# A delta-rule stage in which matmuls of constants are placed by another count

## The chip, the cores and the metric

The kernel runs on one core of a Trainium2 chip. The metric is the time of one launch on the device, in microseconds (us). PE is TensorE's matmul unit and PEld its loading of weights, DVE is VectorE, ACT ScalarE, POOL GpSimd, and SP the engine whose queue issues the DMAs. The clock granted to PE has two levels, 1.2 and 2.4 GHz; the profile gives it as a share of the higher one.

## The reference

Two blocks stand behind each other. The first has two layers on 256 context and 256 latent tokens of width 1024: each is a half FFN, a mixer and a second half FFN, with modulated norms. Layer 0's mixer is the gated delta rule, layer 1's a windowed attention. The second block has a mixer of three branches, a cross-attention to a memory of 256 tokens and an MLP. The change lies in the delta rule:

```python
def _gated_delta_chunked(q, k, v, g, beta):
    ...
    gc = jnp.cumsum(_to_chunks(g, DN_CHUNK), axis=-1)
    decay = jnp.exp(jnp.where(causal, gc[..., :, None] - gc[..., None, :], -jnp.inf))
    kb = k * beta[..., None]
    lower = jnp.where(strict, jnp.einsum('nhcid,nhcjd->nhcij', kb, k) * decay, 0.0)
    rhs = jnp.concatenate([v * beta[..., None], kb * jnp.exp(gc)[..., None]], axis=-1)
    uw = lax.linalg.triangular_solve(lower, rhs, left_side=True, lower=True, unit_diagonal=True)
    ...
    def step(state, inp):
        u_c, w_c, qk_c, qg_c, kd_c, a_c = inp
        v_new = u_c - jnp.einsum('nhik,nhkv->nhiv', w_c, state)
        o = jnp.einsum('nhik,nhkv->nhiv', qg_c, state) + jnp.einsum('nhij,nhjv->nhiv', qk_c, v_new)
        state = state * a_c[..., None, None] + jnp.einsum('nhjk,nhjv->nhkv', kd_c, v_new)
        return state, o
```

There are 8 heads of 128, each run forwards and backwards over 512 tokens.

## The kernel before

All instructions are issued by a planner that runs when the program is built (`Driver`, line 191 is the call through which every operation is recorded). Pieces of work are Python generators: streams with a priority, and jobs, which are taken one after the other and carry the large weight matmuls. The planner keeps a clock of its own for each engine (`Clocks.t`), adds a cost of its own for each operation, and lets the first stream go on whose inputs are ready by these clocks; where none can, the job goes on, and where the job can't either, PE's clock is moved to the next time at which something can (`Driver.run`). So the costs and the constants of the planner set the order of the instructions on each engine; on the chip the engines run these orders and wait for each other by semaphores. Weights in float32 are split into a high and a low part (ACT casts, DVE subtracts, `split_w`, line 433), and products of them are three matmuls each.

The delta-rule stage, as far as it matters here: `dn_subst` loads the diagonal 32x32 blocks of four heads' lower triangles (bx<-ld) and an identity (bx<-in_eye), and `dn_steps` inverts them on DVE in 31 steps of two operations. `dn_head` then loads these inverses (t<-xd) and the triangles (t<-ld), and widens the inverse to 64 and to 128 rows by small matmuls on PE: products of 32x32, a "solve" of many 32x32 matmuls, and two sets of 64x64; it then loads keys, queries and values (t<-s, t<-q). `dn_chain` runs the state through four chunks of 128 tokens, for two directions of a head, with up to four heads under way: matmuls with a state tile s, 128x128, whose results DVE and ACT take up before the next can start. Heads 0 to 3 go first, heads 4 to 7 behind. `dn_norm` and `dn_finish` norm and gate the result, and the output projection (128x512) follows. Beside this, jobs fill PE: the projections of z and six of the eight products of the memory's keys (`mem_k`, 128x256).

From the end of the projections to the last output projection `drv.hot` holds two constants, a tile of ones and the identity (lines 1635 and 1662). While it does, `keep_busy` may issue a float32 matmul of them, 128x128, whose result nobody reads, into a free PSUM tile:

```python
if self.hot is None or until - now < HOT_GAP or self.clk.cols.get(int(now / TICK), 0) >= HOT_COLS or not self.q["ps"]:
    return False
```

It is called at one place, where no stream and no job can go on.

## Time and profile before

| | |
|---|---|
| median of three runs | 2732.3 us (2727.0 to 2738.47) |
| the profiled execution | 2734.16 us |
| its span | 2732.4 us |
| PE, DVE, ACT, POOL busy | 2654.7, 1929.0, 1258.0, 102.2 us |
| the delta-rule stage's part spoken of here | 640.0 to 833.6 us |

The profile is that of one execution. Times in its rows are us from the start of the span unless marked ns; a row of a timeline merges instructions of one kind that follow each other, and the brackets at its end give the idle time before it and what ended it. A float32 matmul leaves two records on PE and two on PEld. In rows of groups "x" is the number of records.

### The profile page before, as it was taken

What the parts mean: (1) busy time and instruction counts of PE and PEld (TensorE: products, weight loads), DVE (VectorE), ACT (ScalarE), POOL (GpSimd) and SP (SyncE); (2) the same over time, 40 slices, a digit from 0 to 9 for tenths busy, and PEclk for the clock granted to TensorE, in tenths of its full rate; (3) what the DMA queues carried; (4) which work ended last, traced back from release to release, by engine and by line L of the source; (5) the groups of instructions that cost most, each with busy time, mean ns of one, the idle gap of its engine ahead of it and who ended that gap; (6) DMA issues with size and microseconds to landing.
All of it is one profiled execution on the core that took longest, in us unless ns stands there. A gap on an engine that the chain in (4) does not pass through costs nothing.

```text
span 2732.4 us, 45388 instructions
## 1 busy us (share of the span) xinstructions
PE 2654.7 (97%) x17414; PEld 2327.2 (85%) x17414; DVE 1929.0 (71%) x3897; ACT 1258.0 (46%) x2799; POOL 102.2 (4%) x114
## 2 busy tenths in 40 slices
PE   6999999999889999999999998999999899999999
PEld 4888888888788888889888886799978899999999
DVE  4778767887868488876433357775588998986763
ACT  3322236764345322224423245564476667555662
POOL 0000000200010000000000002000010211000000
PEclk8999999999879999999999999999999999999999
DMA  6657732668442455673322222165555444554554
GB/s 247 231 194 254 261 123 97 225 200 226 152 151 89 135 206 210 225 257 104 108 93 95 94 90 85 47 214 184 172 167 165 156 153 172 181 188 160 178 193 139
DMA packets 194058, 452.57 MB, mean 166 GB/s; under 512 B 33472, under 2 KB 78624, under 8 KB 193840
## 3 DMA queue, kind: packets, MB, share of 16 engines
q1 hardware_dynamic: 193840, 449.66, 49.2%
q8 instruction: 137, 2.24, 0.3%
q14 instruction: 81, 0.66, 0.1%
HBM read 418.65 MB, written 30.94 MB: 165 GB/s over the span
## 4 chain that ended last, share of the span: by engine, by line
PE 89%; DVE 5%; ACT 2%; DMA 2%; issue 1%; SPq 1%; POOL 0%; DVEq 0%; ACTq 0%; POOLq 0%
PE ps L191 89%; DVE t L191 2%; ACT t L191 1%; DVE rs L191 1%; DVE n L191 1%; SPq L236 1%; ACT s L191 1%; DMA xres<-in_xT 0%; DVE s L191 0%; DMA bx<-ld 0%; DVE xres L191 0%; DMA t<-in_memT 0%; DVE bx L191 0%; ACT L191 0%; DVE acc L191 0%
## 5 line engine op out<-in xcount | busy, mean ns | idle before, releaser
L191 PE MATMUL ps<-t,t 128*128 128x256 f32 (+4 forms) x14610 | 2386.7, 326 | 34.0 <-DVE t L191 19.6
L191 PEld LDWEIGHTS ps<-t,t 128*128 128x128 f32 (+2 forms) x14610 | 2068.6, 186 | 308.3 <-issue 28.7
L191 DVE TENSOR_TENSOR t<-raw,t 128x512 fp32r<-128x512 f32 x1124 | 736.8, 685 | 76.5 <-ACT t L191 69.9
L191 ACT CAST t<-raw 128x512 fp32r<-128x512 f32 x1124 | 630.4, 610 | 261.9 <-DMA raw<-in_ffn_w 177.9
L191 ACT CAST t<-t 128x512 fp32r<-128x512 f32 (+2 forms) x144 | 68.3, 493 | 438.5 <-DVE t L191 438.3
L191 DVE TENSOR_TENSOR t<-t,ps 128x512 f32<-128x512 f32 (+1 forms) x104 | 64.7, 628 | 240.0 <-PE ps L191 239.9
L191 DVE CUSTOM_DVE_ANT_0 t<-row,bx,c_early 128x1024 bf16<-128x1024 f32 x128 | 163.9, 1281 | 54.2 <-DMA row<-in_ada_r 53.7
L191 DVE SCALAR_TENSOR_TENSOR xres<-ps,modG,xres 128x256 f32<-128x256 f32 x216 | 97.2, 479 | 119.1 <-PE ps L191 118.0
L191 ACT ACTIVATE t<-ps 128x512 f32<-128x512 f32 (+3 forms) x161 | 74.9, 466 | 205.3 <-PE ps L191 195.9
L191 POOL TENSOR_TENSOR t<-t,c_late 128x512 f32<-128x512 f32 (+2 forms) x58 | 68.2, 1194 | 1742.4 <-ACT t L191 1106.9
L191 DVE CUSTOM_DVE_ANT_0 row<-row,bx,c_early 128x1024 f32<-128x1024 f32 x96 | 122.9, 1280 | 1.4
L191 DVE TENSOR_TENSOR t<-t,t 128x512 fp32r<-128x512 f32 (+4 forms) x174 | 95.2, 561 | 39.4 <-ACT t L191 39.0
L191 DVE SCALAR_TENSOR_TENSOR t<-ps,c_late,t 128x254 f32<-128x254 f32 (+3 forms) x176 | 112.0, 637 | 12.1 <-ACT t L191 7.0
L191 PE MATMUL ps<-s,t 128*128 128x128 f32 x512 | 88.3, 323 | 12.7 <-ACT s L191 4.5
L191 ACT COPY t<-ps 128x512 f32<-128x512 f32 (+4 forms) x141 | 57.9, 435 | 83.4 <-PE ps L191 77.5
L191 PEld LDWEIGHTS ps<-s,t 128*128 128x128 f32 x512 | 76.5, 224 | 20.5 <-ACT s L191 7.2
L191 DVE SCALAR_TENSOR_TENSOR xres<-t,c_late,xres 128x256 f32<-128x256 f32 x150 | 87.5, 583 | 3.1
L191 ACT ACT_TABLE_LOAD x58 | 74.4, 1283 | 2.7 <-PE ps L191 1.7
L191 PE MATMUL ps<-c_early,t 128*128 128x128 f32 (+1 forms) x374 | 57.9, 280 | 6.3 <-ACT t L191 3.4
L191 ACT ACTIVATE n<-xres 128x256 f32<-128x256 f32 x90 | 35.9, 414 | 59.9 <-DVE xres L191 58.0
L191 ACT ACTIVATE t<-ps,c_late 128x256 f32<-128x256 f32 (+1 forms) x64 | 37.7, 589 | 54.2 <-PE ps L191 53.9
L191 DVE TENSOR_TENSOR acc<-acc,n 128x256 f32<-128x256 f32 x102 | 42.7, 422 | 27.1 <-ACT n L191 23.9
(181 smaller groups left out, 1378.0 us busy)
## 6 DMA issues: line engine op xcount, KB each, us to landing
raw<-in_ffn_w SPq DMA_DIRECT2D x240, 512.0 KB, 4.3
row<-in_ada_r SPq DMA_DIRECT2D x128, 512.0 KB, 4.4
raw<-in_w_in SPq DMA_DIRECT2D x81, 512.0 KB, 3.5
raw<-in_dn_w SPq DMA_DIRECT2D x33, 512.0 KB, 4.0
raw<-in_w_up SPq DMA_DIRECT2D x32, 512.0 KB, 4.0
raw<-in_w_down SPq DMA_DIRECT2D x32, 512.0 KB, 5.6
raw<-in_ffn_w SPq DMA_DIRECT2D x32, 384.0 KB, 3.6
raw<-in_ada_w SPq DMA_DIRECT2D x16, 512.0 KB, 5.6
```

Of the source, the lines that this page charges most:

```text
L191: r = f(*a, **k)
L236: self.nc.sync.dma_start(out=out, in_=in_)
```

## The change

Where before asks how many columns PE was given in the current one of fixed pieces of the planner's time, the changed planner keeps a list of PE's operations with their columns and sums those that began within the last TICK (a constant of the code). It asks at two places: ahead of every choice of work, where it adds a matmul of the constants if the sum is under HOT_WORK, and in waits of at least HOT_GAP, if it is under HOT_WAIT. In waits the limit was 3600 and the least wait 0.3.

```diff
--- before.py
+++ after.py
@@ -44,8 +44,8 @@
 FG = 1
 NWY = 14
 SPLP = 6
-HOT_COLS = 3600
-HOT_GAP = 0.3
+HOT_WORK, HOT_WAIT = 4000, 5500
+HOT_GAP = 0.25
 HOT_LAG = 1.0
 TICK = 3.4133
 DMA_LAT = 0.75
@@ -110,6 +110,7 @@
     def __init__(self):
         self.t = {"PE": 0.0, "ACT": 0.0, "DVE": 0.0, "POOL": 0.0, "DMA": 0.0}
         self.log = {}
+        self.recent = deque()
         self.cols = {}
 
     @staticmethod
@@ -135,6 +136,7 @@
         if e == "PE":
 
             tick = int(start / TICK)
+            self.recent.append((start, cost * 2400 * rows))
             self.cols[tick] = self.cols.get(tick, 0) + cost * 2400 * rows
             if self.cols.get(tick - 1, 0) < 3060:
                 cost *= 2
@@ -337,6 +339,8 @@
     def run(self):
         while True:
             now = self.t["PE"]
+            if self.keep_busy(now, HOT_WORK):
+                continue
             first = [s for s in self.streams if s.split] if self.ahead < AHEAD else []
             for s in first + self.streams:
                 if self.ok(s, now, s in first):
@@ -372,24 +376,26 @@
                 cand = [c for c in cand if c > now]
                 if not cand:
                     raise RuntimeError("no stream can go on: " + self.state())
-                if not self.keep_busy(now, min(cand)):
+                if min(cand) - now < HOT_GAP or not self.keep_busy(now, HOT_WAIT):
                     self.t["PE"] = min(cand)
 
-    def keep_busy(self, now, until):
-
-        if self.hot is None or until - now < HOT_GAP or self.clk.cols.get(int(now / TICK), 0) >= HOT_COLS or not self.q["ps"]:
+    def keep_busy(self, now, least):
+
+        r = self.clk.recent
+        while r and r[0][0] < now - TICK:
+            r.popleft()
+        if self.hot is None or sum(c for _, c in r) >= least:
             return False
         i = next((i for i in self.q["ps"] if all(o[4] <= now - HOT_LAG for o in self.clk.log.get(f"ps{i}", ()))), None)
         if i is None:
             return False
-        self.q["ps"].remove(i)
-        self.q["ps"].appendleft(i)
-        t = self.take("hot")
-        a, b = self.hot
-        self.pe.matmul(t[:, 0:P], a, b, start=True, stop=True)
-        self.free(t)
-        self.q["ps"].remove(i)
-        self.q["ps"].appendleft(i)
+        for _ in range(2):
+            self.q["ps"].remove(i)
+            self.q["ps"].appendleft(i)
+            if _ == 0:
+                t = self.take("hot")
+                self.pe.matmul(t[:, 0:P], *self.hot, start=True, stop=True)
+                self.free(t)
         return True
 
     def state(self):
```

By the order of the instructions, PE has 77 matmuls of the constants in place of 32 (in the rows `c_early` holds the identity). Since they move the planner's clock, other work changes places too. Lines below the diff's first part stand two further down in the changed kernel (L193 for L191, L238 for L236). Three places are shown.

PE, the memory's key products at the start of the stage. Before (ps is a PSUM tile, t a tile of weights or of the normed memory, three matmuls to a group):

```order
L191 MATMUL ps_5785<-t_5928,t_5656 128x256 x2
L191 MATMUL ps_5785<-t_5928,t_5657 128x256
L191 MATMUL ps_5973<-c_early,ones 128x128
L191 MATMUL ps_5785<-t_5933,t_5656 128x256 x2
L191 MATMUL ps_5785<-t_5933,t_5657 128x256
L191 MATMUL ps_5785<-t_5952,t_5682 128x256 x2
L191 MATMUL ps_5785<-t_5952,t_5683 128x256
L191 MATMUL ps_5995<-c_early,ones 128x128
L191 MATMUL ps_5785<-t_5957,t_5682 128x256 x2
L191 MATMUL ps_5785<-t_5957,t_5683 128x256
```

Of the change, the same work, up to the first 32x32 products of head 0:

```order
L193 MATMUL ps_5785<-t_5936,t_5656 128x256 x2
L193 MATMUL ps_5785<-t_5936,t_5657 128x256
L193 MATMUL ps_5989<-c_early,ones 128x128
L193 MATMUL ps_5785<-t_5941,t_5656 128x256 x2
L193 MATMUL ps_5785<-t_5941,t_5657 128x256
L193 MATMUL ps_5997<-c_early,ones 128x128
L193 MATMUL ps_5785<-t_5966,t_5682 128x256 x2
L193 MATMUL ps_5785<-t_5966,t_5683 128x256
L193 MATMUL ps_6010<-c_early,ones 128x128
L193 MATMUL ps_6013<-t_5825,t_5829 32x32 x8
L193 MATMUL ps_6014<-t_5826,t_5830 32x32 x8
L193 MATMUL ps_6031<-c_early,ones 128x128
```

Before, 11 groups of key products stand ahead of head 0's 32x32 products, with two matmuls of the constants among them; now five groups, with four.

PE, the last 64x64 set of one head and the first 32x32 products of the next, among the heads 4 to 7 (n holds a product that is passed on, s a state tile). Before:

```order
L191 MATMUL ps_6961<-t_6848,n_6960 64x64 x4
L191 MATMUL ps_6962<-t_6849,n_6960 64x64 x4
L191 MATMUL ps_7099<-s_7103,t_5846 128x128
L191 MATMUL ps_7118<-t_6947,t_6951 32x32 x8
L191 MATMUL ps_7119<-t_6948,t_6952 32x32 x8
L191 MATMUL ps_7099<-s_7136,t_5850 128x128
L191 MATMUL ps_7150<-s_7105,t_5857 128x128
L191 MATMUL ps_7150<-s_7105,t_5856 128x128
L191 MATMUL ps_7118<-t_6949,n_7070 32x32
```

Of the change:

```order
L193 MATMUL ps_7165<-t_7067,n_7122 64x64 x4
L193 MATMUL ps_7166<-t_7068,n_7122 64x64 x4
L193 MATMUL ps_7335<-s_7311,t_5865 128x128
L193 MATMUL ps_7335<-s_7311,t_5864 128x128
L193 MATMUL ps_7341<-t_7262,t_7266 32x32 x8
L193 MATMUL ps_7342<-t_7263,t_7267 32x32 x8
L193 MATMUL ps_7359<-c_early,ones 128x128
L193 MATMUL ps_7361<-c_early,ones 128x128
L193 MATMUL ps_7363<-c_early,ones 128x128
L193 MATMUL ps_7365<-c_early,ones 128x128
L193 MATMUL ps_7367<-c_early,ones 128x128
L193 MATMUL ps_7335<-s_7369,t_5866 128x128
```

Five matmuls of the constants, into one PSUM tile, stand behind the 32x32 products, ahead of the state matmuls that followed them. Strings of eight stand at four more places: two around the first column sums of the keys' norms, one some 20 rows ahead of head 4's first 32x32 products, and one behind those of head 7.

SP's queue, where the load of the identity for heads 4 to 7 stands (raw is a buffer for weights as they come, bx the tiles of the substitution, s and q scratch in DRAM). Before:

```order
L236 DMA bx_5949<-ld_119 128x32x32
L236 DMA raw_6006<-in_dn_w_out 128x512
L236 DMA raw_6094<-in_dn_w_out 128x512
L236 DMA raw_6192<-in_dn_w_out 128x512
L236 DMA bx_5950<-in_eye 128x1024
L236 DMA t_5817<-s_146 128x512
L236 DMA t_5818<-s_147 128x512
L236 DMA t_5821<-s_148 128x512
L236 DMA t_5822<-s_149 128x512
L236 DMA t_5823<-q_122 128x512
L236 DMA t_5824<-q_123 128x512
```

Of the change:

```order
L238 DMA bx_5948<-ld_119 128x32x32
L238 DMA raw_6089<-in_dn_w_out 128x512
L238 DMA t_5825<-s_146 128x512
L238 DMA t_5826<-s_147 128x512
L238 DMA t_5829<-s_148 128x512
L238 DMA t_5830<-s_149 128x512
L238 DMA t_5831<-q_122 128x512
L238 DMA t_5832<-q_123 128x512
L238 DMA raw_6175<-in_dn_w_out 128x512
L238 DMA bx_5949<-in_eye 128x1024
L238 DMA raw_6257<-in_dn_w_out 128x512
```

The load bx<-in_eye stood behind three loads of weights; now it stands behind one, six loads of head 0 and another of weights.

## Rows read from the trace of the kernel before

**Rows 1.** The page, part 2: PE busy and granted clock in 40 slices, in tenths.

```profile
PE   6999999999889999999999998999999899999999
...
PEclk8999999999879999999999999999999999999999
```

**Rows 2.** Stretches of the stage: length, busy by engine (instructions), granted clock, DMA share, GB/s.

```profile
640.00:654.00 14.00, 12.80 (x68) 9.19 (x66) 6.56 (x18) 5.16 (x12) 0.00 (x0) 1.00 1.07 276
654.00:661.10 7.10, 6.76 (x27) 5.88 (x28) 5.78 (x16) 3.31 (x9) 0.00 (x0) 0.52 1.08 280
...
691.00:705.00 14.00, 10.12 (x152) 8.50 (x152) 12.43 (x33) 6.25 (x20) 1.04 (x1) 1.00 0.79 280
705.00:729.10 24.10, 22.70 (x164) 21.12 (x165) 17.00 (x58) 6.00 (x21) 2.11 (x2) 0.58 0.33 87
729.10:749.60 20.50, 17.80 (x174) 16.11 (x175) 18.16 (x60) 6.58 (x22) 0.00 (x0) 1.00 0.49 145
749.60:777.00 27.40, 27.35 (x267) 24.75 (x262) 12.89 (x42) 8.35 (x28) 2.08 (x2) 0.50 0.50 155
777.00:796.90 19.90, 16.34 (x212) 14.14 (x210) 13.55 (x44) 10.81 (x44) 1.04 (x1) 1.00 0.53 159
796.90:804.30 7.40, 5.13 (x76) 4.85 (x78) 1.81 (x9) 3.83 (x18) 0.00 (x0) 0.54 0.25 73
804.30:833.60 29.30, 26.11 (x227) 23.59 (x220) 25.68 (x84) 16.36 (x58) 7.12 (x7) 1.00 0.26 83
833.60:860.00 26.40, 26.40 (x135) 22.07 (x136) 21.76 (x54) 12.51 (x37) 2.91 (x2) 1.00 0.32 110
640.00:833.60 193.60, 171.83 (x1725) 152.54 (x1723) 136.99 (x412) 79.25 (x261) 14.55 (x14) 0.84 0.55 160
```

**Rows 3.** Chain of waits in the stage: start, length, what.

```profile
664.68 8.59 DMA bx<-ld
...
747.89 20.36 PE ps L191 x223
```

**Rows 4.** Timeline of weight loads, 643 to 658 us: start, length, instruction, idle before it.

```profile
644.18 0.30 PEld L191 LDWEIGHTS ps<-c_early,ones 128*128 128x128 f32 x2 [0.25 <-PE ps L191]
...
651.82 0.30 PEld L191 LDWEIGHTS ps<-c_early,ones 128*128 128x128 f32 x2 [0.25 <-PE ps L191]
...
655.87 0.50 PEld L191 LDWEIGHTS ps<-c_early,ones 128*128 128x128 f32 x2 [0.35 <-PE ps L191]
...
657.58 0.50 PEld L191 LDWEIGHTS ps<-c_early,ones 128*128 128x128 f32 x2 [0.35 <-PE ps L191]
```

**Rows 5.** Timeline of PE: the string of 16, two at half clock, one wait.

```profile
643.74 8.57 PE L191 MATMUL ps<-c_early,ones 128*128 128x128 f32 x32
...
723.74 1.49 PE L191 MATMUL ps<-c_early,ones 128*128 128x128 f32 x4
...
799.17 0.87 PE L191 MATMUL ps<-t,t 32*32 32x32 f32 x16 [3.84 <-ACT t L191]
```

**Rows 6.** Groups of PE from 729.1 and from 749.6 us: count, busy, mean ns, idle before.

```profile
L191 PE MATMUL ps<-s,t 128*128 128x128 f32 x104 | 14.1, 284 | 2.6 <-DVE t L191 2.4
...
L191 PE MATMUL ps<-s,t 128*128 128x128 f32 x66 | 17.2, 440 | 0.1
```

**Rows 7.** Groups of PE by form in the whole stage.

```profile
L191 PE MATMUL ps<-t,t 128*128 128x256 f32 x144 | 21.8, 301 | 0.0
```

**Rows 8.** Timeline of the SP queue, 665 to 681 us.

```profile
665.55 4.77 SPq L236 DMA_DIRECT2D raw<-in_dn_w_out  x1
...
676.99 0.33 SPq L236 DMA_DIRECT2D raw<-in_dn_w_out  x1
677.37 0.42 SPq L236 DMA_DIRECT2D bx<-in_eye  x1
677.88 2.34 SPq L236 DMA_DIRECT2D t<-s  x4
680.27 0.91 SPq L236 DMA_DIRECT2D t<-q  x2
```

## The prediction

> **What bounds the kernel now.** I read the page's slices first: TensorE (PE) is busy 90% or more in nearly every slice of the 2732.4 us span, and its granted clock is below full in two slices of the delta-rule stage [rows 1]. Then the stretches of that stage, cut where the granted clock changes [rows 2]: from 640.0 to 833.6 us the clock is 0.84 in the mean, so at (1 - 0.84) x 2 x 193.6 = 62 us one of the two levels is granted that is half (0.50, which is 1.2 GHz), and from the single stretches 6.8 + 20.2 + 27.4 + 6.8 = 61.2 us. PE is busy 171.8 of the 193.6 us there, so it stands idle for 21.8. Behind the stage it has no idle time (26.40 of 26.40 us), so what the stage gains or loses is gained or lost by the kernel.
>
> Who is late inside the stage differs. Up to about 705 us the chain of waits passes through the SP queue, two DMAs and DVE's substitution steps for heads 4 to 7; then, with few breaks, through PE [rows 3]. The half-clock stretch from 749.6 to 777.0 us has DVE busy for 12.89 of 27.4 us and PE for all of it: there PE's clock sets the pace. From 654.0 to 661.1 us DVE is busy 5.78 of 7.1 us, and from 705.0 to 729.1 us 17.00 of 24.1 us: there a full clock can win no more than 1.3 and 7.1 us, whatever PE does.
>
> **The change, part by part.** The program holds 32 of the constant matmuls before and 77 now. 23 became 34 up to the third 32x32 solve (691 us before); 8 became 27 from there to the first 32x32 products of head 4 (741 us); none became 13 up to the end of head 7's; 1 became 3 behind it. All carry on PE, and nothing is taken away.
>
> *Price of one.* Before runs a string of 16 at full clock: weight loads start from 644.18 to 651.82, 14 steps, 0.546 us each; each waits 0.25 us for the matmul ahead of it, because a string writes one PSUM tile over and over. At half clock (655.87 to 657.58, two steps) a step is 0.855 us and the wait 0.35 [rows 4]; two at 723.74 us take 1.49 [rows 5]. So 45 more cost 24.6 us at full clock and 38.5 at half; where PE would have waited, nothing.
>
> *What a full clock is worth.* Matmuls with a state tile take 284 ns in a full-clock stretch and 440 in a half-clock one, and 104 of them fit in 20.5 us against 66 (and two solves) in 27.4 [rows 6]. The ceiling is half of the 61.2 us, 30.6 us. The Trainium skill, page "TensorE: Matmul & The Clock Gate", section "Terms", puts the penalty at the throttled time times the missing share of the clock, which is this ceiling; by it alone the estimate is -30.6 + 24.6 = -6 us. The trace does not allow all of it, by the DVE figures above.
>
> *640 to 691 us.* Three more stand ahead of the column sums that wait for DVE's acc, where the old string left 0.28 us of waiting: 3 x 0.546 - 0.28 = 1.4 us on the chain. The other eight stand beside the DMA and DVE work that is late there; between 0 and 4.4 us, taken as 0, since PE is not in the chain. The clock there gives back at most 1.3, taken as 0.9. Sum +0.5 us.
>
> *691 to 749.6 us.* The cross-attention keys' products, 144 matmuls in 21.8 us [rows 7], are issued in 48 groups of three, 0.46 us each. Before, 47 stand ahead of the third solve; now 30. So 17 groups, 7.8 us, move behind it, into a part where PE is late; the waits they leave ahead of it are off the chain. PE was busy 10.12 + 22.70 + 17.80 = 50.6 of 58.6 us [rows 2]. With a full clock all the way that is 50.6 - 10.1 = 40.5, with the moved groups 48.3, with 19 more constants (10.4) 58.7. That is the whole stretch with no wait left in it; before there were 8.0 us of waits on DVE and ACT, and I keep half: +4 us. Ends: 0 (all waits filled) and +16 (clock as before, constants at 0.855).
>
> *749.6 to 804.3 us.* PE was busy 27.35 + 16.34 + 5.13 = 48.8 us, 34.2 us of the stretch at half clock. Fully cured: 48.8 - 17.1 = 31.7, plus 13 x 0.546 = 38.8, plus the 5.9 us of waits = 44.7 against 54.7, -10 us. Not cured: 13 x 0.855 = 11.1, less at most 5.9 of waits, +5 us. The last eight come behind the 3.84 us wait for ACT [rows 5], not in it, so they can't mend the clock that falls in it; the eight at the first of head 4's solves and the five at the third lie before and within the long stretch. I take two thirds of the half clock as gone: -11.4, plus 13 x (0.546 x 2/3 + 0.855 / 3) = 8.4, less 3 of waits: -6 us. The ends are -16 (waits filled too) and +5.
>
> *Behind 804.3 us.* Two more constants, 1.1 us, against 29.30 - 26.11 = 3.2 us of idle time: 0.
>
> *The SP queue.* The load of the identity blocks (bx<-in_eye), which DVE's 62 substitution steps wait for, was the fourth entry behind bx<-ld, after three weight loads, and went out at 677.37 because the third of those waited for DVE to empty a buffer until 676.99. Now it is the ninth, behind two weight loads and six loads for head 0. By the rows of before [rows 8] the first weight load goes at 670.3, the six take 2.34 + 0.91 = 3.25 us, and the second could go at once: 674.4; if it waits as the third did, 680.6. So -3 to +3 us on the start of the steps, taken as 0.
>
> Sum: 0.5 + 4 - 6 + 0 + 0 = -1.5 us. The profiled execution took 2734.16 us (its span and 1.8 around it), 1.9 above the median of the three runs, so 2732.7 by its own time and 2731 by the median. About 0.5% (13.7 us) is what a measurement of this kernel can tell from no change; the forecast is no change.
>
> **Rivals.**
> *A, the clock holds and the waits fill.* The constants then stand where PE waited anyway. 640 to 691 gives -1, the next stretch 0, the third -16, the end -1: -18 us, 2714 by the median. For it: the old string of 16 kept 1.00 for its whole length [rows 2, 4]. Against it: strings of eight now also stand between pieces of work, where four times 4.4 us is ready work delayed.
>
> *B, slower: the strings meet a clock that is already half.* A string of four at 655 us and two of them at 723.7 us ran at half clock and did not end it by themselves [rows 2, 4, 5]. If the clock falls where it fell before, each new string costs 0.855 us apiece with nothing back: +2, +16, +5, +1, together +24 us, 2756 by the median. It decides from about half of the 61 us left at half clock: then 15 us come back, and 45 constants at about 0.7 us (31.5) with the moved groups (7.8) cost 17.5 more than the 21.8 us of waits can take up. The Trainium skill, same page, section "A second HAM failure mode: psum-queue depth-cycling", says that short idles between groups of matmuls on PSUM tiles make the clock swing; a string with 0.25 us of waiting in each step is such a case, and by that rule it would not hold the clock at all. The trace of before speaks against this at full clock: 1.00 from 640 to 654 us with 16 in a string.
>
> *C, the SP queue decides.* Had the second weight load to wait for a buffer that the delayed key groups free later, the substitution steps would start 3 us late, and heads 4 to 7 with them; later in the queue two weight loads now also stand ahead of head 5's loads. +3 to +6 us, 2736. For it: three such loads held SP from 665.55 to 677.32 us before [rows 8]. Against it: head 4 also needs room from heads 0 to 3.
>
> **How the numbers follow.** The exchange as summed 0.58, A 0.17, B 0.13, C 0.12. The first and C are within 0.5%; A is faster, and most of B is slower, with a tail of the exchange on each side that I leave out as equal. So faster 0.17, same 0.70, slower 0.13. The range reaches A's end and, above, three quarters of the way to B: 2713 to 2750. The exchange alone would be 2722 to 2743.
>
> **What would show it.** Right: 154 records of the constant on PE in the stage instead of 64 (a matmul leaves two, 32 in the string of 16), spaced 0.55 us in strings; the stage's mean clock above 0.90; its idle time on PE down from 21.8 us to 10 to 15; its length within 10 us of 193.6. The term from 691 to 749.6 us is wrong if head 4's first products start before 738 us. The one behind is wrong if the clock there is all full or still half for 30 us. A shows as a clock of 0.97 or more with a stage under 180 us, B as a clock of 0.85 or less with steps of 0.855 us in the strings, C as bx<-in_eye issued at 680 us or later. A move that starts behind the stage, among the later layers, would be none of these; their order changes only in small swaps.

## The result, and the profile after

| | before | after |
|---|---|---|
| median, four runs each | 2730.7 us (2727.0 to 2738.5) | 2770.3 us (2769.0 to 2770.6) |
| ratio | | 1.0144, 95% interval 1.0122 to 1.0165 |
| span of the profiled execution | 2732.4 us | 2767.0 us |
| PE busy | 2654.7 us | 2682.3 us |

The changed kernel is slower by 39.6 us, and lies 20 us above the range. The page's slices show no new gap: PE is as full as before, and of its clock the two digits in the stage have changed places [rows 1].

```profile
PE   6999999999889999999999999999999999999999
...
PEclk9999999999789999999999999999999999999999
```

The profiled spans differ by 34.6 us, and the stage has nearly all of it. Its stretches on the changed kernel, cut again where the granted clock changes, between the same two places as the last row but one of [rows 2] (from the start of the stage to the last output projection; columns as there):

```profile
639.10:678.70 39.60, 35.36 (x376) 28.57 (x375) 26.16 (x58) 15.45 (x40) 1.04 (x1) 1.00 1.03 272
678.70:687.00 8.30, 8.30 (x59) 7.44 (x57) 4.61 (x18) 3.42 (x11) 0.00 (x0) 0.59 0.58 200
...
696.80:707.00 10.20, 9.80 (x62) 9.16 (x62) 5.04 (x16) 2.37 (x8) 0.17 (x1) 0.52 0.53 176
...
720.20:747.20 27.00, 25.52 (x99) 20.02 (x98) 14.58 (x47) 2.54 (x8) 1.29 (x1) 0.50 0.39 107
...
768.00:779.00 11.00, 10.60 (x41) 8.42 (x42) 2.34 (x10) 1.74 (x5) 0.00 (x0) 0.53 0.01 2
779.00:815.90 36.90, 29.97 (x391) 25.62 (x390) 23.59 (x77) 16.37 (x64) 2.08 (x2) 1.00 0.52 165
815.90:839.70 23.80, 21.89 (x155) 18.36 (x156) 7.12 (x29) 6.94 (x28) 5.07 (x5) 0.50 0.30 100
839.70:865.10 25.40, 21.45 (x155) 18.77 (x153) 20.12 (x64) 12.54 (x44) 2.04 (x2) 1.00 0.10 32
639.10:865.10 226.00, 197.66 (x1810) 167.40 (x1808) 136.91 (x411) 78.69 (x260) 14.63 (x14) 0.83 0.47 138
```

226.0 us stand against 193.6, so 32.4 more. PE's idle time did not fall to 10 to 15 us, it rose from 21.8 to 226.00 - 197.66 = 28.3. The mean clock is 0.83, not above 0.90: by the five stretches and some tenths beside them 78.5 us were granted 1.2 GHz, against 61.2 before. The groups by form show which matmuls the time went to (count of records | busy us, mean ns of one | idle us ahead of them). After:

```profile
L193 PE MATMUL ps<-s,t 128*128 128x128 f32 x478 | 82.4, 318 | 9.8 <-DVE t L193 3.7 <-ACT s L193 3.6 <-ACT t L193 1.3
L193 PE MATMUL ps<-c_early,ones 128*128 128x128 f32 x154 | 47.3, 399 | 4.1 <-DVE t L193 0.6
L193 PE MATMUL ps<-t,t 128*128 128x256 f32 x144 | 25.1, 312 | 2.0 <-ACT t L193 2.0
```

and the constants of before, which [rows 7] did not show:

```profile
L191 PE MATMUL ps<-c_early,ones 128*128 128x128 f32 x64 | 16.6, 347 | 1.3
```

The 45 added constants are 90 more records and 30.7 us more of PE's busy time, with 2.8 us more of waiting ahead of them; the state matmuls, at 83.4 us before, took 1.0 us less and the key products [rows 7] 3.3 us more. So by the profile alone the constants' own time is as large as nearly all of the 32.4 us; the runs below give a good third of the loss to something else. The timeline of PE shows where they stand, with the wait of [rows 5] behind the fourth of them:

```profile
722.52 6.77 PE L193 MATMUL ps<-c_early,ones 128*128 128x128 f32 x16 [0.42 <-DVE t L193]
...
736.95 6.77 PE L193 MATMUL ps<-c_early,ones 128*128 128x128 f32 x16 [0.17 <-DVE t L193]
...
767.86 6.64 PE L193 MATMUL ps<-c_early,ones 128*128 128x128 f32 x16
...
793.82 2.67 PE L193 MATMUL ps<-c_early,ones 128*128 128x128 f32 x10
...
817.35 0.87 PE L193 MATMUL ps<-t,t 32*32 32x32 f32 x16 [3.89 <-ACT t L193]
818.15 6.77 PE L193 MATMUL ps<-c_early,ones 128*128 128x128 f32 x16
```

Four strings of eight run at half clock (in the third it fell during the first step). The steps inside the first one, and inside the string of five at 793.82 us, are those of [rows 4], in the same view of weight loads:

```profile
722.52 0.50 PEld L193 LDWEIGHTS ps<-c_early,ones 128*128 128x128 f32 x2 [0.61 <-DVE t L193]
723.38 0.50 PEld L193 LDWEIGHTS ps<-c_early,ones 128*128 128x128 f32 x2 [0.35 <-PE ps L193]
...
793.82 0.30 PEld L193 LDWEIGHTS ps<-c_early,ones 128*128 128x128 f32 x2
794.37 0.30 PEld L193 LDWEIGHTS ps<-c_early,ones 128*128 128x128 f32 x2 [0.25 <-PE ps L193]
```

A string at half clock takes 0.85 us for each constant, and the clock did not rise at its end: the first two lie inside 27.0 us at 0.50, and the clock rose some 4, 4 and 15 us behind the ends of the last three. The five at 793.82 us ran at full clock and cost 0.545 each. Where the time was added, by the starts of the same instructions in both timelines, with the time that the granted clock stood at half between them:

| from, to | before | after | added | forecast | at half clock, before and after |
|---|---|---|---|---|---|
| stage start to head 3's first 32x32 products | 640.0 to 701.3 | 639.1 to 707.2 | 6.8 | | 6.8, 17.1 |
| to head 4's | 741.3 | 752.4 | 5.2 | +4.5 for these two rows | 20.5, 27.3 |
| to head 7's solve | 803.3 | 826.1 | 11.8 | -6 | 33.2, 20.5 |
| to the end of the stage | 833.6 | 865.1 | 8.6 | 0 | 1.0, 13.6 |
| to the last column sums of the kernel | 2548.0 | 2582.9 | 3.4 | 0 | 17.1, 23.9 |

The third row is the only one in which the time at half clock fell. Its stretch before, then after, in the columns of [rows 2], and the constants in the second:

```profile
741.30:803.30 62.00, 53.71 (x576) 47.95 (x576) 34.70 (x116) 24.52 (x94) 3.12 (x3) 0.73 0.43 129
```

```profile
752.40:826.10 73.70, 61.16 (x639) 50.45 (x637) 36.04 (x116) 26.98 (x101) 3.12 (x3) 0.86 0.40 123
```

```profile
L193 PE MATMUL ps<-c_early,ones 128*128 128x128 f32 x42 | 15.0, 457 | 1.1
```

No constant stood there before. The 21 of the change took 15.0 us, the rest of PE's work took 7.6 us less, and PE's idle time rose from 8.3 to 12.5 us.

On SP's queue the identity blocks went out 3.9 us sooner than before [rows 8]. Yet the first substitution step began 3.2 us later, because DVE's queue ahead of it stood in a state operation's wait. DVE's timeline before, then after:

```profile
681.47 0.19 DVE L191 TENSOR_TENSOR n<-bx,bx 128x31 f32<-128x31 f32 x1 [2.47 <-DMA bx<-in_eye]
```

```profile
683.27 0.35 DVE L193 SCALAR_TENSOR_TENSOR s<-ps,dn_cA,t 128x128 f32<-128x128 f32 x1 [2.89 <-issue]
...
684.66 0.17 DVE L193 TENSOR_TENSOR n<-bx,bx 128x31 f32<-128x31 f32 x1
```

From the first step to the last, DVE then waited 9.4 us for PE in place of 0.9, and the result, xd<-bx, went out at 737.25 us in place of 724.89. Further on, the third store of the memory's keys stood at the head of the queue for 15.9 us:

```profile
673.50 0.39 SPq L238 DMA_DIRECT2D bx<-in_eye  x1
...
737.25 0.37 SPq L238 DMA_DIRECT2D xd<-bx  x1
...
762.74 0.91 SPq L238 DMA_DIRECT2D t<-q  x2
779.53 0.32 SPq L238 DMA_DIRECT2D kxd<-t  x1
```

### The profile page after: what moved, and what is told of

The parts are those of the page before. It is cut to its first block, busy times and chain, and to the rows that moved or that the text cites. A ratio compares the mean times of both kernels' runs of the same rounds, so it can differ in the third digit from the quotient of the medians.

```text
span 2767.0 us, 45535 instructions
## 1 busy us (share of the span) xinstructions
PE 2682.3 (97%) x17504; PEld 2343.9 (85%) x17504; DVE 1929.9 (70%) x3897; ACT 1257.2 (45%) x2799; POOL 101.2 (4%) x114
## 4 chain that ended last, share of the span: by engine, by line
PE 91%; DVE 4%; ACT 2%; DMA 1%; issue 1%; SPq 0%; POOL 0%; DVEq 0%; ACTq 0%; POOLq 0%
PE ps L193 91%; DVE t L193 2%; ACT t L193 1%; DVE n L193 1%; DVE rs L193 1%; ACT s L193 1%; DVE s L193 0%; DMA xres<-in_xT 0%; ACT L193 0%; SPq L238 0%; DMA t<-csd 0%; DMA raw<-in_ada_w 0%; DVE xres L193 0%; DMA raw<-in_ffn_w 0%; DMA t<-s 0%
## 5 line engine op out<-in xcount | busy, mean ns | idle before, releaser
L193 PE MATMUL ps<-t,t 128*128 128x256 f32 (+4 forms) x14610 | 2391.4, 326 | 39.0 <-DVE t L193 20.2
L193 PEld LDWEIGHTS ps<-t,t 128*128 128x128 f32 (+2 forms) x14610 | 2069.4, 186 | 312.2 <-issue 27.6
L193 DVE TENSOR_TENSOR t<-raw,t 128x512 fp32r<-128x512 f32 x1124 | 737.3, 686 | 73.8 <-ACT t L193 67.6
L193 ACT CAST t<-raw 128x512 fp32r<-128x512 f32 x1124 | 631.1, 610 | 261.4 <-DMA raw<-in_ffn_w 188.0
L193 ACT CAST t<-t 128x512 fp32r<-128x512 f32 (+2 forms) x144 | 68.2, 493 | 434.0 <-DVE t L193 433.7
L193 DVE TENSOR_TENSOR t<-t,ps 128x512 f32<-128x512 f32 (+1 forms) x104 | 64.7, 628 | 234.3 <-PE ps L193 234.2
L193 DVE CUSTOM_DVE_ANT_0 t<-row,bx,c_early 128x1024 bf16<-128x1024 f32 x128 | 163.9, 1280 | 52.9 <-DMA row<-in_ada_r 52.4
L193 DVE SCALAR_TENSOR_TENSOR xres<-ps,modG,xres 128x256 f32<-128x256 f32 x216 | 97.2, 479 | 118.3 <-PE ps L193 117.4
L193 ACT ACTIVATE t<-ps 128x512 f32<-128x512 f32 (+3 forms) x161 | 74.9, 466 | 200.3 <-PE ps L193 192.8
L193 POOL TENSOR_TENSOR t<-t,c_late 128x512 f32<-128x512 f32 (+2 forms) x58 | 67.3, 1173 | 1742.8 <-ACT t L193 1124.4
L193 DVE CUSTOM_DVE_ANT_0 row<-row,bx,c_early 128x1024 f32<-128x1024 f32 x96 | 122.9, 1280 | 1.4
L193 DVE TENSOR_TENSOR t<-t,t 128x512 fp32r<-128x512 f32 (+4 forms) x174 | 95.2, 561 | 39.5 <-ACT t L193 39.3
L193 DVE SCALAR_TENSOR_TENSOR t<-ps,c_late,t 128x254 f32<-128x254 f32 (+3 forms) x176 | 112.0, 637 | 11.7 <-ACT t L193 6.6
L193 ACT COPY t<-ps 128x512 f32<-128x512 f32 (+4 forms) x141 | 58.3, 434 | 90.3 <-PE ps L193 84.2
L193 PE MATMUL ps<-s,t 128*128 128x128 f32 x512 | 88.0, 316 | 9.9 <-ACT s L193 3.7
L193 PEld LDWEIGHTS ps<-s,t 128*128 128x128 f32 x512 | 75.9, 219 | 17.5 <-ACT s L193 6.2
L193 DVE SCALAR_TENSOR_TENSOR xres<-t,c_late,xres 128x256 f32<-128x256 f32 x150 | 87.2, 581 | 3.1
L193 PE MATMUL ps<-c_early,t 128*128 128x128 f32 (+1 forms) x374 | 60.7, 286 | 11.6 <-ACT t L193 6.5
L193 PEld LDWEIGHTS ps<-c_early,t 128*128 128x128 f32 (+1 forms) x374 | 43.5, 145 | 28.7 <-ACT t L193 14.6
L193 ACT ACTIVATE s<-ps,dn_cV 128x128 f32<-128x128 f32 x64 | 23.1, 368 | 93.7 <-DVE s L193 62.4
L193 ACT ACTIVATE n<-xres 128x256 f32<-128x256 f32 x90 | 36.0, 414 | 59.8 <-DVE xres L193 57.9
```

The costliest lines, as they stand in the source:

```text
L193: r = f(*a, **k)
```

## The experiments

Three theories stood against each other. Theory 1: constants between pieces of work cost their own time on PE. Theory 2: the changed order of the other work costs by itself. Theory 3: constants in waits earn time by holding the clock. A constant that is "planned, not issued" moves the planner's clock and leaves no instruction, so that the order of all other instructions stays. The results, with the ratio to before and its interval:

| kernel | median us (range) | ratio |
|---|---|---|
| after's order, 53 constants between work not issued | 2742.8 (2740.9 to 2749.8) | 1.0058 (1.0037 to 1.0079) |
| after's order, no constant issued | 2745.8 (2742.5 to 2754.6) | 1.0070 (1.0042 to 1.0098) |
| after's order, strings on one PSUM tile | 2748.2 (2744.8 to 2750.6) | 1.0074 (1.0046 to 1.0102) |
| after's order, the 53 issued twice | 2779.5 (2775.4 to 2784.7) | 1.0190 (1.0164 to 1.0216) |
| before's order, no constant issued | 2730.8 (2723.0 to 2735.0) | 1.0011 (0.9996 to 1.0027) |
| before, strings on one PSUM tile | 2728.9 (2722.0 to 2736.5) | 0.9998 (0.9980 to 1.0016) |
| before's order and 45 constants more | 2743.4 (2743.0 to 2746.1) | 1.0061 (1.0044 to 1.0077) |
| rolling count in waits only, planned anew | 2740.6 (2740.1 to 2747.3) | 1.0048 (1.0035 to 1.0061) |
| lag test mended, planned anew | 2749.9 (2740.4 to 2754.2) | 1.0073 (1.0051 to 1.0095) |

### The constants themselves

**53 between pieces of work planned, not issued.**

```diff
         if i is None:
             return False
+        if least == HOT_WORK:
+            ...
+            self.end(self.clk.run("PE", self.pe.cost("matmul", (o, a, b), {}), [a, b], [o]))
+            return True
         for _ in range(2):
```

> The changed kernel with its order of instructions kept on every engine; the 53 constant matmuls that the planner adds between work are planned but not issued, the 24 in waits are. Theory 1 (the constants' own time on PE, 0.855 us a step at half clock in four strings of eight, ahead of work that is ready): some 33 us go, 2737 us against 2770. Theory 2 (the moved order: key groups, SP's loads): at most 8 us go, 2762 or more. Theory 3 (the constants do hold the clock and without them it falls longer): more than 60 us at half clock beyond the 78 of the changed kernel, 2770 or more.

27.5 us come back, 0.52 apiece: theory 1. But 12 us and more stay, with 24 constants issued where before has 32.

**None issued** (the same, without the condition).

> As the run before, but none of the 77 constants is issued. Theory 1: a little below the run with 24, 2730 to 2737 us, since the 24 stand where PE waits anyway. Theory 2: 2760 or more. Theory 3: slower than the run with 24 by 5 us or more, since these too keep the clock.

The two medians lie 3 us apart and their intervals overlap, so the 24 in waits earn little if anything. What stays, 15 us or more over before, is the order alone, if the 32 constants of before earn nothing either (see below).

**Strings on one PSUM tile**, taken once, so that no step waits for the one ahead of it.

```diff
+        t = self.last.get(i)
+        if t is None or self.hot_t.get(i) is not t:
+            t = self.hot_t[i] = self.take("hot")
+            self.free(t)
...
         self.pe.matmul(t[:, 0:P], *self.hot, start=True, stop=True)
```

> The changed kernel with the same order and all 77 constants, but a string takes one PSUM tile once and writes it over without a wait on the matmul ahead. A step should take about 0.27 us at full and 0.53 at half clock, as matmuls with a state tile do, in place of 0.546 and 0.855. Theory 1: the cost of 33 us falls to 15 to 20, 2750 to 2757 us, less if the denser strings end the half clock sooner. Theory 2: 2765 or more.

The time lies just under theory 1's range, on the side that it left open for denser strings. PE's timeline of that kernel, the first two strings of eight:

```profile
721.05 3.78 PE L193 MATMUL ps<-c_early,ones 128*128 128x128 f32 x16 [0.40 <-DVE t L193]
...
731.50 3.78 PE L193 MATMUL ps<-c_early,ones 128*128 128x128 f32 x16 [1.56 <-DVE t L193]
```

A string of eight at half clock takes 3.78 us, not 6.77, and the kernel is 22 us faster than the changed one with the same 77 constants in the same places. The 77 now cost 2.4 us over none at all (2748.2 against 2745.8) where they cost 24.5 with the waits in their steps. The loss by the constants is thus the waits inside the strings, more than the matmuls: a part of it is PE's time in the steps, and a part the clock, which stood at half for 47.8 us in this stage, not for 78.5; each of the four strings now ends within 2 us of the end of its half-clock stretch. One execution of each was profiled, but the granted clock of every run is on record: (1 - clock) x 2 x span gives 119 us at half clock over the whole span in the mean of the changed kernel's four runs (105 to 138), and 88 in the four on one tile (60 to 104). How much of the 22 us this is, they do not say. In the prediction I set aside a rule of the Trainium skill, page "TensorE: Matmul & The Clock Gate", section "A second HAM failure mode: psum-queue depth-cycling", that short idles between groups of matmuls make the clock swing; the page tells it of bf16 matmuls that cycle through PSUM's banks. At half clock these two kernels fit it: with the waits, the strings did not mend the clock; without them, the time at half clock is 31 us shorter. At full clock the trace still speaks against it: the changed kernel's first string, of 19 with such waits, stands in a stretch of 39.6 us at 1.00.

**The 53 issued twice**, the second into the other half of the tile.

```diff
                 self.pe.matmul(t[:, 0:P], *self.hot, start=True, stop=True)
+                if least == HOT_WORK:
+                    self.pe.eng.matmul(t[:, P:2 * P], *self.hot, start=True, stop=True)
```

> The changed kernel with the same order, each of the 53 constants between work issued twice, the second into other columns of the same tile with no wait ahead of it: 53 more at 0.27 us (full clock) to 0.53 (half). Theory 1: 14 to 28 us slower than the changed kernel, 2784 to 2798. Theory 2: no change, 2770. Theory 3: the denser strings keep the clock, faster than 2765.

53 more cost 9.2 us over the changed kernel, 0.17 apiece, a third of the first 53 and less than theory 1's 14 to 28. In the timeline of weight loads (L399 is the added one) a pair at half clock takes 1.28 us where one took 0.85: the second waits for nothing and adds 0.43 us, and the wait of 0.35 us stays, now for the second. Why it cost 0.17 and not 0.43 is not shown.

```profile
721.60 0.50 PEld L193 LDWEIGHTS ps<-c_early,ones 128*128 128x128 f32 x2 [0.35 <-PE ps L399]
721.98 0.55 PEld L399 LDWEIGHTS ps<-c_early,ones 128*128 128x128 f32 x2
722.88 0.50 PEld L193 LDWEIGHTS ps<-c_early,ones 128*128 128x128 f32 x2 [0.35 <-PE ps L399]
```

### The order

**Before's order, its 32 constants planned and not issued.**

> The order of the kernel before, with its 32 constants planned and not issued. Theory 2: 2727 to 2735 us, at least 10 under the 2745.8 that the changed order without any constant took, which leaves the order alone as the difference between the two. Theory 1 alone (the order costs nothing, what stays is the missing hold on the clock): 2740 to 2748, the same as the changed order without any. Theory 3 (the constants in waits earn time by holding the clock): at least 4 us slower than before, 2731 or more; if they earn nothing, within 3 us of before.

Theory 2: 15.0 us lie between two kernels that differ in the order alone. For theory 3 the ratio leaves 3 us, between -1 and +7: what the 32 constants earn can't be told from nothing. They do hold the clock a little: 28 runs of the kernel before, taken beside these ten, had 88 us at half clock in the mean (60 to 115), these 109 (76 to 131). Half of the 21 us is the most that this can be worth.

**Before, strings on one PSUM tile** (the edit as above, in the kernel before).

> The kernel before, its order and its 32 constants, but a string keeps one PSUM tile taken once, so that no step waits for the one ahead of it. In the changed kernel this took a string of eight from 6.7 to 3.8 us. Theory 1 (a constant costs its time on PE where PE is late, and nothing in a wait): 0 to 4 us under before, 2723 to 2727, since the 32 stand mostly in waits. Theory 3 (they hold the clock in waits): the string of 16 at the start of the stage shrinks from 8.6 to about 4.3 to 6 us and leaves a longer wait; if the clock then falls sooner than at 654 us, 2 to 6 us slower than before, 2729 to 2733.

No difference, to within some 5 us: in waits, how long a constant takes was no matter.

**Before's order word for word, and 45 constants more**, which a rolling count adds between pieces of work unseen by the planner's clock.

```diff
             now = self.t["PE"]
+            self.unseen(now)
...
+    def unseen(self, now):
+        ...
+        while self.hot is not None and self.q["ps"] and sum(c for _, c in r) < HOT_WORK:
+            ...
+            self.pe.eng.matmul(t[:, 0:P], *self.hot, start=True, stop=True)
+            ...
+            r.append((now, 512))
```

> The order of the kernel before, word for word, with its 32 constants, and 45 more that the rolling count adds between pieces of work without telling the planner's clock: 77 in all, as in the changed kernel, 20 of them between the third 32x32 solve and head 4's first products. Theory 1 (constants between pieces of work cost their own time on PE, 0.55 us apiece at full clock and 0.855 at half, less what they fill): 45 x 0.55 to 0.855 = 25 to 38, less some 5 to 8 of waits: 2745 to 2758 us. Theory 2 (the changed order costs 15 us by itself and adds to that): this kernel stays 10 us or more under the changed kernel's 2770. A rival (there is no order effect apart from the constants): within 5 us of 2770.

In before's order the 45 constants cost 15 us over the kernel before of the same runs (2728.2; 0.34 apiece), and the kernel stays 27 us under the changed one. So the order adds its 15 us, and 77 constants cost 24.5 us in the changed order (2770.3 - 2745.8) against 12.6 in that of before (2743.4 - 2730.8). The sum: 15.0 + 12.6 + 11.9 for both together = 39.5 us, by medians of different runs, in which the kernel before took 2726.6 to 2733.6. The 11.9 us are not the order's doing alone: the constants stand in other places here, behind the third 32x32 solve one string of seven and otherwise at most four, where the changed kernel has four strings of eight. Their hold on the clock shows, too: 78 us at half clock in the mean of the four runs (60 to 104), against 109 without constants, and yet they cost more than they gave back.

**The rolling count in waits alone** (`HOT_WORK` is 0), planned anew.

> The rolling count in waits alone (HOT_WORK is 0): 29 constants in the stage, none between pieces of work, and the planner orders the rest by itself. Theory 1 (the constants between pieces of work cost their own time on PE, and that is the loss): the loss goes, 2722 to 2738 us. Theory 2 (some 16 us of the loss come from the order in which the other work now stands, whatever causes it): an order planned with a rolling count in waits is also another order, so anything from 2727 to 2750 is possible, and the key groups tell: if 45 or more of the 48 stand ahead of the third 32x32 solve as before, 2727 to 2735. Theory 3 (the constants in waits hold the clock, and 29 hold it as well as 32 did): a mean clock of 0.82 to 0.86 from the projections' end to the output projection.

Above theory 1's range. No constant stands between work, all key products are ahead of head 3 as before, and it is 13.7 us slower than before (2726.9 in these runs) all the same: a third order that costs. How much of it the order takes is not separated here.

**HOT_LAG's test mended.** In both kernels the test looks up a name that is in no log (`f"ps{i}"`; the log's names are those of whole tiles), so that it never keeps a constant out of a tile that is still being read; the planner then books a stall, its sum lapses, and it adds seven more. That is how the strings of eight arise.

```diff
-        i = next((i for i in self.q["ps"] if all(... self.clk.log.get(f"ps{i}", ()))), None)
+        i = next((i for i in self.q["ps"] if all(... self.clk.log.get(self.last[i].tensor.tag if i in self.last else "", ()))), None)
```

> The changed kernel with keep_busy's test of HOT_LAG made to find the PSUM tile's last operations: a constant goes only into a tile whose reader has been done for 1 us by the planner's clocks. 44 constants in place of 77, in tiles that take turns, singles and pairs from the third 32x32 solve on, no string of eight there. Theory 1: 33 constants fewer at 0.55 to 0.855 us, so 18 to 28 us under the changed kernel, 2742 to 2752, and less the more of them stand in waits. Theory 2: the planner orders the rest anew; 17 key groups of three moved behind the third solve, as in the changed kernel, keep it at 2740 or more. A rival (the strings' place does not matter, the count does not either, the clock does): within 6 us of 2770.

20 us come back with 33 constants fewer, and 20 by the ratio stay over before. Both theories have their part.

### What in the order costs

All of these issue no constant, so they stand against 2745.8 us (after's order) and 2730.8 (before's), 1.0070 and 1.0011 as ratios.

| kernel | median us (range) | ratio to before |
|---|---|---|
| after's order, 39 key matmuls behind head 3 left out | 2752.0 (2743.7 to 2753.5) | 1.0083 (1.0063 to 1.0103) |
| before's order, the same 39 left out | 2731.8 (2726.4 to 2739.5) | 0.9999 (0.9982 to 1.0015) |
| after's order, the 39 ahead of head 3 instead | 2749.3 (2741.1 to 2750.4) | 1.0061 (1.0040 to 1.0083) |
| after's order, no substitution steps for heads 4 to 7 | 2733.1 (2722.4 to 2738.3) | 1.0010 (0.9997 to 1.0023) |
| before's order, the same | 2715.7 (2714.5 to 2718.2) | 0.9958 (0.9943 to 0.9972) |
| after's rule up to head 3's first products, then before's | 2762.0 (2761.2 to 2763.7) | 1.0109 (1.0086 to 1.0132) |
| before's rule up to there, then after's | 2729.3 (2724.1 to 2735.4) | 0.9995 (0.9981 to 1.0010) |
| after's order, two weight loads behind head 3's loads | 2745.1 (2744.2 to 2750.5) | 1.0069 (1.0047 to 1.0090) |
| after's order, no wait for the third store of keys | 2744.8 (2742.3 to 2748.7) | 1.0046 (1.0030 to 1.0062) |

**The key products, three kernels.** Matmuls in the middle of a group are planned and not issued; in the third kernel ten earlier groups are issued two or three times over.

```diff
+                    drv.skip = 4 * KD + 2 <= i * KD + k < 6 * KD
...
-        mm = self.drv.pe.matmul
+        mm = self.drv.pe.planned if self.drv.skip else self.drv.pe.matmul
```

> The changed kernel's order without any constant (2745.8 us), with 39 of the 42 matmuls of key products left out that stand behind head 3's first 32x32 products there (planned, not issued; so the keys are not the reference's). If the price of the changed order is that these products now stand where PE is late: 39 x 0.15 to 0.29 = 6 to 11 us come back, 2735 to 2740. If the price is DVE's queue (the substitution steps of heads 4 to 7 stand behind more instructions that wait for PE and ACT): less than 4 us, 2742 or more.

> The order of the kernel before without any constant (2730.8 us), with the same 39 matmuls of key products left out, which there stand ahead of head 3's first 32x32 products (so the keys are not the reference's). Theory 2a (these matmuls stand in PE's waits there and cost nothing): 2727 to 2732 us. Theory 2b (in their old places they keep PE's clock up for the state matmuls, which is why leaving them out behind head 3 brought nothing): 2736 or more. Theory 2c (they are PE time wherever they stand): 2720 to 2725, 6 to 11 us less.

> The changed kernel's order without any constant (2745.8 us), the 39 matmuls of key products left out behind head 3's first products, and 39 earlier ones issued twice, so that as many stand ahead of the first products of heads 0, 1, 2 and 3 (561, 594, 642 and 669) as in the order of before (561, 594, 642, 672); the keys are not the reference's. If the moved key products are the order's price: 2730 to 2736 us. If something else in the order is: 2743 or more, as without the 39 (2752.0).

Nothing came back in the first, the second lost nothing (theory 2a), and putting as many matmuls back ahead of head 3 brought nothing. The groups that I priced at 7.8 us in the prediction are not the order's price.

**The substitution steps, in both orders.**

```diff
-            drv.dve.tensor_tensor(out=tv, ...)
+            sub = drv.dve.tensor_tensor if b == 0 else drv.dve.planned
+            sub(out=tv, ...)
```

> The changed kernel's order without any constant (2745.8 us), with the 62 substitution steps of heads 4 to 7 left out on DVE (planned, not issued; these heads' inverses are identities). If the order's price comes by way of these steps (their result, xd<-bx, went out 9 us later than in the order of before): at least 8 us come back beyond what the same cut brings in the order of before, 2730 or less, and the two orders differ by under 7 us. If the steps are not on the path that sets the end, both orders gain alike (some 24 us of DVE's time, of which PE's waits take a part), and stay 10 us or more apart.

> The same cut in the order of the kernel before, without any constant (2730.8 us): 62 substitution steps of heads 4 to 7 left out on DVE. The difference to the kernel with the changed order and the same cut is what tells: under 7 us if the order's price comes by way of the steps, 10 us or more if not. By itself: 2715 to 2729.

Both gain, by 12.7 and 15.1 us, and they stay 17.4 apart: the steps' time is not the order's price. The cut separates less than I meant it to, since xd<-bx stands on SP's queue behind head 3's loads, and these went out late in the changed order. SP's timeline there, then that of before's order with the same cut:

```profile
716.72 0.91 SPq L243 DMA_DIRECT2D t<-q  x2
717.67 0.43 SPq L243 DMA_DIRECT2D xd<-bx  x1
```

```profile
706.91 0.90 SPq L241 DMA_DIRECT2D t<-q  x2
707.86 0.43 SPq L241 DMA_DIRECT2D xd<-bx  x1
```

**One half of the order each.** A flag set at head 3's first products changes the rule of both kinds of constants.

```diff
-            if self.keep_busy(now, HOT_WORK):
+            if not self.late and self.keep_busy(now, HOT_WORK):
...
+        drv.late = drv.late or h >= 3
```

> None of the constants issued. The changed planner's rule and so its order up to head 3's first 32x32 products, the rule of before from there on. If the order's price of 15 us arises ahead of head 3's first products (the substitution's result was 9 us late): 2742 us or more. If it arises behind: 2735 or less. The part behind is ordered anew, which may add some us by itself, as the rolling count in waits did (2740.6).

> None of the constants issued. The rule of before and so its order up to head 3's first 32x32 products, the changed rule from there on. If the order's price arises ahead of head 3's first products: 2728 to 2735 us. If it arises behind: 2742 or more.

The price goes with the order ahead of head 3's first products, whichever rule follows; the part behind is planned anew in both kernels, so they are halves of the rule and not of the order word for word. With before's order up to there the kernel is as fast as before, although there the substitution's result goes out 92.5 us behind that of heads 0 to 3 (92.7 in after's order, 84.0 in before's). So a late xd<-bx is not the price by itself. The other half is 16 us worse than the changed order, so that the part behind can cost as well; in it head 3's loads stand behind xd<-bx on SP's queue, and go out 90.7 us behind the first xd<-bx, in after's order 77.4:

```profile
732.94 0.38 SPq L240 DMA_DIRECT2D xd<-bx  x1
733.42 4.73 SPq L240 DMA_DIRECT2D t<-s  x4
738.20 0.91 SPq L240 DMA_DIRECT2D t<-q  x2
```

**Two single places on SP's queue.** First the two weight loads ahead of head 3's loads, held until these are issued:

```diff
-            fin, c.at = self.fin, self.dma(c.raw[:, :c.n], c.ap)
+            fin, c.at = self.fin, self.dma(c.raw[:, :c.n], c.ap, self.outs in (5, 6) and ...)
...
             drv.dma(qk[d], self.qdd[h][d])
+        drv.flush()
```

> The changed kernel's order without any constant (2745.8 us), with two weight loads (raw<-in_dn_w_out) on SP's queue moved behind head 3's loads (t<-s x4, t<-q x2), which stood behind them; all other engines' orders are the same. The loads then go out some 4.6 us sooner, 72 to 73 us behind the first xd<-bx, as in the order of before. If these loads' place on SP's queue is the price of the order: 2730 to 2738 us. If only their own delay is given back: 2739 to 2743. If head 3's loads are not on the path that sets the end: 2744 or more.

No change: head 3's loads went out 75.6 us behind the first xd<-bx, 1.8 sooner, since without the two loads ahead SP stood 12.0 us in a wait for PE there.

Then the third store of the memory's keys, which held SP in the changed kernel:

```diff
-        drv.dma(self.kxd[:, 2 * h:2 * h + 2, :], ...)
+        for j in (h, 2) if h == 1 else (h,):
+            ...
```

> The changed kernel's order without any constant (2745.8 us), with the third store of the memory's keys issued right behind the second, from the second's tile (so this pair of keys is not the reference's): SP's queue no longer waits there for these keys; all other engines' orders are the same. In the trace of the unchanged order SP stood 9.6 us at that store, and head 6's loads and then head 5's, of which the latter waited for buffers for 5 us more, stood behind it. If the store's place is the price of the order: 2730 to 2737 us. If it is a part of it, as far as head 5's loads can start sooner (5 us): 2738 to 2742. If head 5's loads wait for the buffers of earlier heads anyway: 2744 or more.

The median is 1.0 us lower; by the ratios, whose intervals overlap, 6.6 us came back. So the runs leave open whether the store's place costs nothing or some part of the order's price. The trace speaks for little: SP now stands at the next entry: head 6's inverses wait for buffers, and head 5's loads go out 135.1 us behind the first xd<-bx, with the store in its place 134.4.

```profile
755.88 10.62 SPq L240 DMA_DIRECT2D t<-xd  x2
766.60 3.36 SPq L240 DMA_DIRECT2D t<-ld  x2
775.08 1.76 SPq L240 DMA_DIRECT2D t<-s  x4
```

These loads could not start sooner, since another wait stood right behind the one taken out.

What is left of the order's price can be read from a view of stretches, cut at two places that all kernels share: the issue of the first xd<-bx, and column sums behind the stage. Before's order without constants, the half with before's order, after's order without constants, and the changed kernel:

```profile
641.87:869.07 227.20, 195.69 (x1896) 174.21 (x1895) 171.27 (x492) 99.35 (x316) 17.35 (x16) 0.88 0.55 161
```

```profile
639.98:877.28 237.30, 207.49 (x1899) 183.41 (x1898) 170.91 (x493) 99.48 (x316) 17.71 (x16) 0.84 0.52 154
```

```profile
642.08:885.98 243.90, 207.26 (x1899) 183.35 (x1898) 172.58 (x493) 99.69 (x316) 17.46 (x16) 0.85 0.51 150
```

```profile
638.59:908.49 269.90, 241.53 (x2053) 204.94 (x2052) 172.03 (x493) 99.92 (x316) 17.55 (x16) 0.85 0.45 135
```

The first three run the same work, and PE idles for 31.5, 29.8 and 36.6 us (36.1 in the kernel without the third store). So some 5 to 7 us of the price is PE waiting. In the fourth it idles for 28.4: the constants fill 8 us of waits and add 34 us of busy time. The rest shows as the same matmuls taking longer at a lower clock; but the second row has that too, and its kernel's median is as low as the first's. The clock differs that much between kernels whose medians are equal, so one execution of each can't carry this part.

The clock on record of all runs carries it further. In three pairs of kernels that differ in the order alone, the changed order stood longer at half clock in the mean: 132 us against 109 without constants, 162 against 131 with the 39 key matmuls left out, 104 against 71 without the substitution steps (4 to 10 runs each). Half of the difference, 12 to 17 us, is the most that it can cost; with the 5 to 7 us of waits that is enough for the 15, 20 and 17 us between the medians. It is no proof: before's order without the 39 matmuls had as much half clock as after's order in full, 131 and 132 us, and is 14 us faster; and the runs of most of these kernels differ by 30 us and more among themselves. Which entries ahead of head 3's first products make the difference stays open.

No kernel that does all of the work beats the kernel before beyond its interval.

## Why the prediction was wrong

**The price and the number of constants were right.** 154 records stand where 64 stood, the steps are 0.545 and 0.855 us, and the 45 added 30.7 us to PE, between the 24.6 and 38.5 that I worked out.

**The step that failed is what the clock gives back.** "I take two thirds of the half clock as gone" and, for 691 to 749.6 us, "with a full clock all the way" turned a cost into -6 and +4. By these two and the 0.9 us before them some 16 us at half clock should have been left of 61; there were 78.5. The sum took strings of eight as holding or mending the clock. They met a clock that was at half or fell in their first step, and did not mend it as long as each step waited for the one ahead. By the clock on record, over whole spans, the 77 constants took 13 us of half clock from the changed order (119 in the mean of four runs, 132 without any), which the spread (104 to 160) can't tell from nothing. I had this before me: the constants at 655 and 723.7 us [rows 4, 5] were such cases, and the string of 16 that held the clock stood at full clock and in a wait.

In the term of -6 itself, heads 4 to 7, the time at half clock did fall, by 12.7 of 33.2 us and not by two thirds. There the other two parts of the term were off as well: 15.0 us for 21 constants in place of 8.4 for 13, and 4.3 us more of waits in place of 3 less. With 7.6 us less of other work on PE that makes 11.7.

Rival B named the mechanism; its condition, more than half of the 61 us left at half clock, came true, with its steps of 0.855 us and a stage clock of 0.83. I gave it a chance of 0.13.

**Rival B's own price was too small by 15 us**, because it moved the constants and priced the rest of the order by the moved key products alone. The order costs 15 us without any constant and these products have no part in it that the runs show. The constants cost more in the changed order and its places, too: 12 us over the 77. The term behind 804.3 us is a case of it: two constants, I wrote, against 3.2 us of idle time, so 0. It became 8.6, since the half clock that fell in the wait for ACT lasted 23.8 us, through the string behind that wait and on into work that had 1.00 before [rows 2].

**640 to 691 us.** Forecast +0.5; 6.8 up to head 3's first products. I took what stands beside late DMA and DVE work as free; by the kernels with half of the rule, the 15 us go with the order of this part.

**The SP queue.** The load bx<-in_eye went out 3.9 us sooner, and rival C's sign did not come. But the term was for the start of the steps, taken as 0, and they began 3.2 us later, just outside its -3 to +3: it had the wait on SP's queue and left out the one on DVE's. They ended 12.4 us later, since DVE's queue puts more work between them that waits for PE (9.4 us of waits in place of 0.9).

**Two places in the order were named wrongly.** The string of eight that I put some 20 rows ahead of head 4's first products stands ahead of head 5's (767.86 us), so 8 of the 27 constants that I counted ahead of head 4 belong to the next term; that moves 4 to 7 us from one term to the other and leaves the sum. And the second piece of the order sets before's products of head 5 beside those of head 6 of the change.

## What to carry to other kernels

A matmul that only keeps the engine busy cost nothing that could be measured in a wait here, and 0.52 us, most of its step of 0.545 to 0.855, ahead of ready work; ask for each string whether the clock is still full where it will run, and write it so that its steps don't wait for each other. Price a change to a planner's clock as two changes, the instructions it adds and the new order of all the others: plan them and don't issue them, and the order's part can be measured alone. Before taking a long wait at the head of a queue for a price, look at what the next entry in it could have started sooner.

## What the runs showed of the hardware

Strings of eight with a wait of 0.35 us in each step, at half clock, ran inside a stretch of 27.0 us that was granted 0.50 throughout, with PE busy for 25.5 of them. With the same constants on one tile the step at half clock fell from 0.855 to 0.47 us (3.78 us for eight), and a second constant into the other half of the tile, with the waits, added 0.43 us to the step of 0.855 and left its wait of 0.35 as it was. And one profiled execution says little about a kernel's clock: between the same two places the stage without constants ran at 0.88 with before's order and at 0.84 with half of it, in kernels whose medians differ by 1.5 us and whose ten runs each had 109 and 106 us at half clock in the mean.
